# First layer's conditioning weights in pieces of 512 columns, and a charge for narrow tiles in the order planner

## The chip, the core and the metric

The kernel runs on one core of a Trainium2 chip: TensorE (PE, with its weight loads as PEld), VectorE (DVE), ScalarE (ACT), GpSimd (POOL) and SyncE (SP), which issues all DMAs. The metric is the device time of one execution in microseconds (us), the median of three runs.

## What is computed

Two layers of a hybrid mixer over 128 context tokens and 512 latent tokens, model width 2048, all in float32. The part that matters here is the start of a layer:

```python
mod_lat = (jax.nn.silu(c) @ w_ada[l] + b_ada[l])     # w_ada[l]: 2048 x 6144: shift, scale, gate
h = rmsnorm(x, norm_pre[l]) * (1.0 + scale) + shift
... = split_cols(h @ w_in[l])                        # 2048 x 6368
```

So `h`, and with it every product of the layer, waits for the scale and the shift, and these are a vector (one for context, one for latent tokens) times 2048 x 2048 weights each. What follows (a gated delta rule over 8 heads, latent attention over 4 heads, pooling over 4 groups, the output projection) is untouched by the change.

## The kernel before

**Order.** Every instruction is first recorded by `Sched.record`, with a cost from `Sched.cost`, and then placed by `Sched.run`, a list scheduler: each engine takes the ready instruction of highest priority in a simulated time, and the order in which it took them is the order of the program on that engine. `either` leaves a choice between two engines, which the scheduler settles by whichever is free first (the rounding `copy` between ACT and DVE, the remainder `rest` between POOL and DVE). So a change of a cost moves instructions all over the program. All instructions are emitted from one line (L499 in the profile), hence groups are told apart by tiles.

**The start of layer 0.** `start` goes over the 2048 columns of scale (`kind` 1) and shift (`kind` 0) in pieces listed in `WSTART`: eight of 256 columns. A piece and kind is loaded in four DMAs of 512 KB, each four row blocks of 128 rows by 256 columns (rows of 1 KB), alternately into the tiles `aw0` (slabV) and `aw1` (slabW), four buffers each. There are 64 such loads; they are numbered 1 to 64 here in program order. `ada_rows` multiplies each row block: the stationary operand is the conditioning vector as 128 x 32, so a product uses only 32 of the 128 output columns of the array, and row block `i` writes rows `32*(i % 4)` of one PSUM bank. Four row blocks thus use four different quarters of the array. `ada_sum` evacuates the sums, transposes them (tag `hp0`, a single PSUM bank) and adds up the four quarters; `mod_cols` makes `acl` and `bcl` from them. After the first piece the tokens `x` are loaded and normalised (`xnorm`), and for each 128 columns `k` of a finished piece `h_tile` transposes the tokens on PE (also in bank `hp0`), scales and shifts them (ACT or DVE) and splits them into a rounded part and a remainder. `consts2`, called after the first piece, transposes the convolution weights and small norms, in the same bank `hp0`; its last transposition (128x20) needs the small load `pool_scale`.

**Work beside it.** The first projections (`win_group` with tag `ax`, six PSUM banks) run over the blocks `k` as they become ready: products of 384 and of 256 columns in fp32r, called wide here. Everything else of the layer follows these.

Of the kernel before, what the change touches and what calls it, by code (L numbers as in the profile page):

```python
# [17 lines left out]
D = 2048  # L18
NK = 16
# [22 lines left out]
DK_EPS = 128 * EPS  # L42
RW = 24384
WW = {"W": 4096, "V": 4480}
WSTART = (256,) * 8
SW = 20248


# [103 lines left out]
def cols(x):  # L152
    n = 1
    for s in x.shape[1:]:
        n *= s
    return n


class Sched:
# [190 lines left out]
    def run(self):  # L350
        self.prepare()
        ev = []
        seq = 0
        engs = ["PE", "DVE", "ACT", "POOL", "SP"]
        free = {e: True for e in engs}
        heap = {e: [] for e in engs}
        hw = 0.0
        bus = 0.0
        last, warm, port = -10.0, 0.0, 0.0

        def push(o):
            for e in {o.eng, *o.alts}:
                heapq.heappush(heap[self.ENG[e]], (o.pr, o))

        for op in self.ops:
            if op.need == 0:
                push(op)
        now = 0.0
        done = 0
        order = []  # L370
        again = []

        def retry(tags):
            for g in tags:
                for o in g.waiting.pop(g.next, ()):
                    o.parked = False
                    push(o)

        every = [g for g in self.tags.values() if g.space != "D"]
        while True:  # L380
            for e in engs:
                while free[e] and heap[e]:
                    pr, op = heapq.heappop(heap[e])
                    if op.placed or op.parked:
                        continue
                    new = [t for t in op.tiles if t.slot is None]
                    miss = None
                    for t in new:
                        if not self.grant(t):
                            miss = t  # L390
                            break
                        if t.tag.space != "D":
                            again.append(t.tag)
                    if miss is not None:
                        op.parked = True
                        miss.tag.waiting.setdefault(miss.n, []).append(op)
                        continue
                    op.placed = True
                    if self.ENG[op.eng] != e:
                        (op.eng, op.meth, op.a, op.k, op.cost, op.lock), = [(n, *x) for n, x in op.alts.items() if self.ENG[n] == e]  # L400
                    op.start = now
                    op.seq = len(order)
                    order.append(op)
                    if op.meth == "dma_start":
                        hw = max(hw, now) + 0.45
                        op.bus = max(bus, hw)
                        bus = op.bus + op.nbytes / 340e3
                        op.end = max(bus, hw + 0.3) + 2.0
                    else:
                        cost = op.cost  # L410
                        if e == "PE":
                            if now - last > 3.4:
                                warm = now + 3.4
                            if now < warm:
                                cost *= 2
                            last = now + cost
                        op.end = now + cost
                        if op.lock:
                            op.end = max(now, port) + cost
                            port = op.end  # L420
                    free[e] = False
                    heapq.heappush(ev, (now + op.cost if op.meth == "dma_start" else op.end, 0, seq, e))
                    heapq.heappush(ev, (op.end, 1, seq, op))
                    seq += 1
            if again:
                retry(again)
                again = []
                if any(free[e] and heap[e] for e in engs):
                    continue
            if not ev:  # L430
                break
            now = ev[0][0]
            rel = False
            while ev and ev[0][0] <= now + 1e-9:
                _, kind, _, x = heapq.heappop(ev)
                if kind == 0:
                    free[x] = True
                elif kind == 1:
                    done += 1
                    eng = self.ENG[x.eng]  # L440
                    for t in x.tiles:
                        t.left -= 1
                        if t.left == 0 and t.tag.space != "D":
                            heapq.heappush(ev, (now + self.FREE[t.tag.space], 3, seq, t))
                            seq += 1
                    for s in x.succ:
                        s.need -= 1
                        lat = self.LAT["DMA" if x.meth == "dma_start" else eng][self.ENG[s.eng]]
                        s.ready = max(s.ready, now + lat)
                        if s.need == 0:  # L450
                            heapq.heappush(ev, (s.ready, 2, seq, s))
                            seq += 1
                elif kind == 3:
                    g = x.tag
                    g.used[x.slot] = None
                    x.dead = True
                    while g.low < len(g.tiles) and g.tiles[g.low].dead:
                        g.low += 1
                    rel = True
                else:  # L460
                    push(x)
            if rel:
                retry(every)
        if done != len(self.ops):
            waits = [(o.i, o.eng, o.meth, [t.tag.name for t in o.tiles if t.slot is None]) for o in self.ops if not hasattr(o, "end") and o.need == 0]
            raise RuntimeError(f"stuck: {done} of {len(self.ops)}: {waits[:5]}")
        self.order = order
# [34 lines left out]
class Body:  # L502
# [5 lines left out]
    def memory(self):  # L508
# [41 lines left out]
                       ("T1", 1, 160), ("T2", 1, 320), ("rv", 2, 128), ("Z", 4, 128), ("kg", 2, 128), ("s", 5, 128), ("dj2", 1, 128)], SW)  # L550
        put("S", fix, [("xy", 5, 2048), ("of", 2, 640), ("junk", 1, 512), ("ssy", 1, 25), ("zb", 6, 1), ("zh", 6, 1), ("zb4", 3, 4), ("gr3", 1, 384), ("G", 2, 1024), ("xr", 3, 512)], SW)
        put("S", at("gr3"), [("sq", 1, 256)], SW)
        st = [("r", 2, 128), ("th", 1, 128), ("ao", 1, 256), ("at3", 1, 4)]
        put("S", SW - sum(n * w for _, n, w in st), st, SW)
        put("S", SW - 260, [("ao2", 1, 256), ("at4", 1, 4)], SW)
        r4 = [at("raw") + 512 * i for i in range(4)]
# [112 lines left out]
    def start(self):  # L669
        nc, a = self.nc, self.a  # L670
        self.x1d = [[self.dram([128, 1024]) for _ in range(2)] for _ in range(NT)]
        r = self.T("r", [96, 128])
# [3 lines left out]
        p = self.ps("hp0")  # L676
# [6 lines left out]
        c0 = 0  # L683
        for s, w in enumerate(WSTART):
            ks = slice(c0 // 128, (c0 + w) // 128)
            n = w // 128
            for kind in (1, 0):
                p = self.ps("ad")
                for kc in range(4):
                    w4 = self.T(f"aw{kc % 2}", [128, 4, w])  # L690
                    nc.sync.dma_start(w4, a["w_ada"][0, kc * 512:(kc + 1) * 512, kind * D + c0:kind * D + c0 + w].rearrange("(k p) n -> p k n", p=128))
                    self.ada_rows(p, w4, kc * 4, kc == 0, kc == 3)
                t2 = self.T("at3", [128, n, 2])
                self.ada_sum(t2, p, self.T("ao", [128, w]), "hp0")
                self.mod_cols(0, kind, ks, t2, acl, bcl)
            if s == 0:
                for t in range(NT):
                    x = self.T("xy", [128, D])
                    nc.sync.dma_start(x, a["x_prompt"][0] if t == 0 else a["x_sample"][0, (t - 1) * 128:t * 128, :])
                    self.xt.append(x)  # L700
                for t in range(NT):
                    self.xnorm(t)
            for k in range(ks.start, ks.stop):
                self.h_tile(0, k, acl, bcl, "hp0")
            if s == 0:
                self.consts2()
            c0 += w
# [746 lines left out]
            nc.vector.scalar_tensor_tensor(szc[:, o0:o0 + n], p[:, :n], self.misc[:, 12 + 4 * l + g:13 + 4 * l + g], szc[:, o0:o0 + n], op0=ALU.mult, op1=ALU.mult)  # L1454
        nc.sync.dma_start(self.od[12 + g], szc)

    def ada_rows(self, p, w, k0, start, stop):

        nc = self.nc
        n = w.shape[1]  # L1460
        for i in range(n):
            j = i % 4
            with nc.later(-20 if i else 0):
                nc.tensor.matmul(p[32 * j:32 * j + 32, :w.shape[2]], self.ccol[:, 2 * (k0 + i):2 * (k0 + i) + 32], w[:, i], start=start and i < 4, stop=stop and i >= n - 4)

    def ada_sum(self, dst, p, o, pst):

# [8 lines left out]
    def ada_cols(self, l, i0, i1, tag, pst, m=1):  # L1476

        nc, a = self.nc, self.a
        for i in range(i0, i1, m):
# [3 lines left out]
            p = self.ps(pst)  # L1483
            for j, w in enumerate(ws):
                with nc.later(-20 if j else 0):
                    self.ada_rows(p[:, 128 * j:128 * j + 128], w, 0, True, True)
            with nc.later(-2):
                s = self.T("at4", [128, m, 2])
                self.ada_sum(s, p, self.T("ao2", [128, 128 * m]), pst)
# [177 lines left out]
```

## Time and profile before

| | us |
|---|---|
| median of three runs (2635.53 to 2638.45) | 2635.76 |
| profiled execution, own time | 2642.71 |
| profiled execution, span of its instructions | 2640.6 |
| PE busy in that span | 2541.0 (96%) |
| DVE, ACT, POOL busy | 1664.4, 1026.8, 739.7 |
| DMA, mean rate over the span; in the first 66 us | 132 GB/s; 314 GB/s |

A busy time is the sum of an engine's instructions, and PE counts as busy while a product is in its pipeline. The profile shows 40 slices of 66 us: PE is at 40% in the first one and at 90% or more in nearly all others; DMA is at 90% or more in the first two and far lower later.

### The profile page before, as it was taken

How to read it: one execution, taken by the hardware profiler on the slowest of the kernel's cores; microseconds unless marked ns; L12 is line 12 of the kernel's file. 1: busy time of each engine (PE TensorE's matmuls, PEld its weight loads, DVE VectorE, ACT ScalarE, POOL GpSimd, SP SyncE). 2: the span in 40 equal slices, each digit the busy share in tenths (PEclk: the TensorE clock that was granted, in tenths of full speed). 3: DMA queues.
4: the chain of work that ended last, by engine and by line, in shares of the span. 5: the costliest groups of instructions: out<-in, count | busy, mean ns of one | idle time of the engine just before them, and what ended most of it. 6: DMA issues, size and time to landing. Idle time of an engine off the chain costs nothing.

```text
span 2640.6 us, 52982 instructions
## 1 busy us (share of the span) xinstructions
PE 2541.0 (96%) x20553; PEld 2380.4 (90%) x20553; DVE 1664.4 (63%) x4229; ACT 1026.8 (39%) x2789; POOL 739.7 (28%) x825
## 2 busy tenths in 40 slices
PE   4999999999999999999988999999999999999998
PEld 1689999999999998878888999999999999988888
DVE  3545556888888886332257365678878887755225
ACT  3233345444444432222247333444444444323222
POOL 0021112354333333220025211233444333334002
PEclk7999999999999999999998999999999999999999
DMA  9944444332343333896755434523433334336225
GB/s 314 335 108 110 133 116 121 96 95 83 92 103 101 102 91 100 235 271 173 190 182 157 126 95 126 149 78 91 101 103 90 91 92 103 84 84 194 92 75 191
DMA packets 541202, 347.98 MB, mean 132 GB/s; under 512 B 103826, under 2 KB 499734, under 8 KB 540310
## 3 DMA queue, kind: packets, MB, share of 16 engines
q1 hardware_dynamic: 540950, 344.59, 46.7%
q8 instruction: 162, 2.65, 0.4%
q14 instruction: 90, 0.74, 0.1%
HBM read 313.07 MB, written 31.46 MB: 130 GB/s over the span
## 4 chain that ended last, share of the span: by engine, by line
PE 80%; DMA 6%; DVE 3%; ACT 2%; POOL 1%; issue 1%; SPq 1%; DVEq 0%; ACTq 0%
PE psum L499 80%; DVE slab L499 3%; DMA slab<-d 2%; DMA slab<-in_w_in_dram 1%; DMA slab<-in_w_ada_dram 1%; ACT slab L499 1%; POOL slabr L499 1%; DMA slabW<-in_w_ada_dram 1%; DMA d<-slab 1%; SPq L499 1%; ACT slabr L499 1%; ACT slabW L499 0%; DMA slab<-in_x_sample_dram 0%; DVE slabV L499 0%; DMA slabW<-d 0%
## 5 line engine op out<-in xcount | busy, mean ns | idle before, releaser
L499 PE MATMUL psum<-slabr 128*128 128x384 f32 (+2 forms) x11760 | 2011.1, 324 | 2.3 <-DVE slabW L499 1.0
L499 PEld LDWEIGHTS psum<-slabr 128*128 128x128 f32 x11760 | 1778.2, 190 | 86.9 <-issue 23.5
L499 POOL TENSOR_TENSOR slabr<-slab,slabr 128x512 fp32r<-128x512 f32 (+3 forms) x428 | 482.8, 1136 | 1200.3 <-ACT slabr L499 878.8
L499 ACT ACTIVATE slabr<-slab 128x512 fp32r<-128x512 f32 (+3 forms) x731 | 393.3, 548 | 879.2 <-PE psum L499 726.5
L499 DVE TENSOR_TENSOR slabr<-slab,slabr 128x512 fp32r<-128x512 f32 (+3 forms) x404 | 262.8, 654 | 416.1 <-ACT slabr L499 363.8
L499 PE MATMUL psum<-slab 128*128 128x128 f32 (+4 forms) x4375 | 434.7, 256 | 56.7 <-DVE slab L499 31.9
L499 DVE TENSOR_TENSOR slab<-slab 128x5 f32<-128x5 f32 (+20 forms) x1298 | 473.2, 376 | 19.2 <-DMA slab<-d 3.9
L499 ACT ACTIVATE slab<-psum 128x128 f32<-128x128 f32 (+6 forms) x823 | 276.1, 351 | 492.5 <-PE psum L499 384.7
L499 PEld LDWEIGHTS psum<-slab 128*128 128x128 f32 (+4 forms) x4375 | 352.1, 140 | 97.5 <-DVE slab L499 39.3
L499 DVE SCALAR_TENSOR_TENSOR slab<-slab 128x5 f32<-128x5 f32 (+7 forms) x618 | 348.2, 572 | 42.9 <-ACT slab L499 33.9
L499 ACT ACTIVATE slab<-slab 128x642 f32<-128x642 f32 (+4 forms) x240 | 141.1, 603 | 62.3 <-DVE slab L499 55.7
L499 DVE COPY slab<-psum 32x160 f32<-32x160 f32 (+9 forms) x214 | 84.0, 399 | 112.7 <-PE psum L499 98.0
L499 DVE TENSOR_SCALAR slab<-slab 128x1 f32<-128x1 f32 (+7 forms) x363 | 111.4, 326 | 29.0 <-ACT slabW L499 16.2
L499 POOL TENSOR_SCALAR slab<-slabV,slab 128x128 f32<-128x128 f32 x128 | 58.1, 460 | 217.5 <-PE psum L499 216.9
L499 DVE SCALAR_TENSOR_TENSOR slab<-psum,slab 128x128 f32<-128x128 f32 (+1 forms) x216 | 80.1, 378 | 56.4 <-PE psum L499 54.5
L499 DVE TENSOR_REDUCE slab<-psum 128x4 f32<-128x16 f32 (+3 forms) x104 | 39.5, 380 | 106.5 <-PE psum L499 105.3
L499 PE MATMUL psum<-slab,slabW 32*32 32x32 f32 (+2 forms) x1216 | 80.8, 219 | 14.5 <-DMA slab<-d 7.8
L499 POOL TENSOR_TENSOR slab<-slab 128x640 f32<-128x640 f32 (+5 forms) x46 | 68.1, 1481 | 95.1 <-ACT slab L499 77.8
L499 ACT ACTIVATE slab<-psum,slab 128x256 f32<-128x256 f32 (+2 forms) x93 | 58.7, 641 | 78.3 <-DVE slab L499 74.6
L499 PEld LDWEIGHTS psum<-slab,slabW 32*32 32x32 f32 (+2 forms) x1216 | 66.3, 132 | 23.1 <-DMA slab<-d 10.7
L499 DVE SCALAR_TENSOR_TENSOR slab<-slab,psum 128x128 f32<-128x128 f32 (+2 forms) x160 | 62.0, 395 | 37.2 <-PE psum L499 25.9
L499 PE MATMUL psum<-slab,slabV 128*128 128x128 f32 (+1 forms) x352 | 72.4, 296 | 1.9 <-DVE slab L499 1.4
(61 smaller groups left out, 1384.5 us busy)
## 6 DMA issues: line engine op xcount, KB each, us to landing
slab<-in_w_in_dram SPq DMA_DIRECT2D x186, 512.0 KB
slab<-in_w_ada_dram SPq DMA_DIRECT2D x32, 1024.0 KB
slabW<-in_w_ada_dram SPq DMA_DIRECT2D x32, 1024.0 KB
slab<-in_w_out_dram SPq DMA_DIRECT2D x64, 512.0 KB
slabW<-d SPq DMA_DIRECT2D x64, 320.0 KB
slabV<-in_w_ada_dram SPq DMA_DIRECT2D x32, 512.0 KB
slabW<-in_w_ada_dram SPq DMA_DIRECT2D x32, 512.0 KB
d<-slab SPq DMA_DIRECT2D x32, 320.0 KB
```

The source lines that it names most:

```text
L499: op.inst = getattr(getattr(nc, op.eng), op.meth)(*[real(x) for x in op.a], **{n: real(x) for n, x in op.k.items()})
```

## The change

`WSTART` becomes three pieces of 512 columns and two of 256. A load stays at 512 KB: for a piece of 512 columns it holds two row blocks (rows of 2 KB) and there are eight per kind, for one of 256 it holds four, as before. The number of loads stays 64; the first 48 are of the new form. `ada_rows` takes the row block's number instead of start and stop flags, so the two row blocks of one load write quarters 0 and 1 or quarters 2 and 3. `ao` and `at3` grow to 512 columns. In `Sched.run` a product on PE counts as narrow when its stationary operand has under 128 rows or 32 columns; a step to a narrow one is charged 0.1 us more, a step back 0.27 us.

```diff
-WSTART = (256,) * 8
+WSTART = (512, 512, 512, 256, 256)
...
                         if e == "PE":
+                            part = op.a[1].shape[0] < 128 or cols(op.a[1]) == 32
+                            if part != narrow:
+                                cost += 0.1 if part else 0.27
+                            narrow = part
...
-        st = [("r", 2, 128), ("th", 1, 128), ("ao", 1, 256), ("at3", 1, 4)]
+        st = [("r", 2, 128), ("th", 1, 128), ("ao", 1, 512), ("at3", 1, 8)]
...
-                for kc in range(4):
-                    w4 = self.T(f"aw{kc % 2}", [128, 4, w])
-                    nc.sync.dma_start(w4, a["w_ada"][0, kc * 512:(kc + 1) * 512, kind * D + c0:kind * D + c0 + w].rearrange("(k p) n -> p k n", p=128))
-                    self.ada_rows(p, w4, kc * 4, kc == 0, kc == 3)
+                m = 1024 // w
+                for i, k in enumerate(range(0, NK, m)):
+                    w4 = self.T(f"aw{i % 2}", [128, m, w])
+                    nc.sync.dma_start(w4, a["w_ada"][0, k * 128:(k + m) * 128, kind * D + c0:kind * D + c0 + w].rearrange("(k p) n -> p k n", p=128))
+                    self.ada_rows(p, w4, k)
...
-    def ada_rows(self, p, w, k0, start, stop):
+    def ada_rows(self, p, w, k0):
...
-            j = i % 4
+            j = (k0 + i) % 4
             with nc.later(-20 if i else 0):
-                nc.tensor.matmul(p[32 * j:32 * j + 32, :w.shape[2]], self.ccol[:, 2 * (k0 + i):2 * (k0 + i) + 32], w[:, i], start=start and i < 4, stop=stop and i >= n - 4)
+                nc.tensor.matmul(p[32 * j:32 * j + 32, :w.shape[2]], self.ccol[:, 2 * (k0 + i):2 * (k0 + i) + 32], w[:, i], start=k0 + i < 4, stop=k0 + i >= NK - 4)
```

The order of PE's instructions shows what this does to the loads' products. The row with `slabV` or `slabW` and a first size of 32 is one load; `slabr` rows are wide products, `slab 128x128` are transpositions. First, PE before, from ahead of load 15 to load 17:

```order
L499 MATMUL psum<-slab 128x120
L499 MATMUL psum<-slabV_78,slab 32x256 x4
L499 MATMUL psum<-slab 128x120
L499 MATMUL psum<-slabW_80,slab 32x256 x4
L499 MATMUL psum<-slabr 128x384 x2
L499 MATMUL psum<-slabr 128x256 x2
L499 MATMUL psum<-slabr 128x384 x6
L499 MATMUL psum<-slabr 128x256 x4
L499 MATMUL psum<-slabr 128x384 x4
L499 MATMUL psum<-slab 128x20
L499 MATMUL psum<-slab 128x128 x2
L499 MATMUL psum<-slabV_78,slab 32x256 x4
```

The last row is load 17: the first 18 wide products stand between loads 16 and 17, and the transposition of 20 rows, which waits for `pool_scale`, behind them. PE in the change, from load 16 (the first row) to load 21:

```order
L503 MATMUL psum<-slabW_80,slab 32x512 x2
L503 MATMUL psum<-slab 128x128 x4
L503 MATMUL psum<-slabV_78,slab 32x512 x2
L503 MATMUL psum<-slabW_80,slab 32x512 x2
L503 MATMUL psum<-slab 128x128 x3
L503 MATMUL psum<-slabV_78,slab 32x512 x2
L503 MATMUL psum<-slab 128x128 x2
L503 MATMUL psum<-slabW_80,slab 32x512 x2
L503 MATMUL psum<-slabr 128x384 x3
L503 MATMUL psum<-slab 128x128 x3
L503 MATMUL psum<-slabV_78,slab 32x512 x2
```

The first wide product stands behind load 20 now; loads 17 and 18 follow each other without anything between, the others here do not. PE in the change, from load 31 to the transposition of 20 rows, which now stands between loads 32 and 33:

```order
L503 MATMUL psum<-slabV_78,slab 32x512 x2
L503 MATMUL psum<-slabr 128x384 x4
L503 MATMUL psum<-slabW_80,slab 32x512 x2
L503 MATMUL psum<-slabr 128x384 x4
L503 MATMUL psum<-slabr 128x256 x12
L503 MATMUL psum<-slabr 128x384 x12
L503 MATMUL psum<-slab 128x20
```

Its load follows load 35 on SP (before: load 22). Counted over PE's whole order: before load 64 is multiplied, 120 wide products of 384 columns and 116 of 256 stand in the order before, 100 and 98 in the change; from load 16 to load 64 there are 87 transpositions and other small products before and 95 in the change; steps from wide to narrow and back come to 74 before and 80 in the change in that stretch, and to 253 and 251 in all that follows load 64. Of the 32 loads of 512 columns that follow load 16, six stand in three groups with a partner next to them (17 and 18; two of 33 to 35; two of 36 to 38). On the other engines 36 remainders of weights move from DVE to POOL.

## Rows read from the trace of the kernel before

**Rows 1.** The page: span, and busy time of each engine.

```profile
span 2640.6 us, 52982 instructions
...
PE 2541.0 (96%) x20553; PEld 2380.4 (90%) x20553; DVE 1664.4 (63%) x4229; ACT 1026.8 (39%) x2789; POOL 739.7 (28%) x825
```

**Rows 2.** Windows: stretch, its length, busy by engine (count), granted clock, DMA share, GB/s.

```profile
0.00:49.00 49.00, 20.76 (x137) 5.77 (x137) 21.00 (x84) 23.32 (x57) 0.47 (x6) 0.72 0.96 321
49.00:67.00 18.00, 11.35 (x77) 6.79 (x73) 3.51 (x12) 3.08 (x6) 2.88 (x5) 0.71 0.97 294
67.00:118.00 51.00, 51.00 (x468) 35.83 (x466) 26.40 (x71) 11.23 (x24) 1.71 (x2) 1.00 1.08 335
118.00:139.00 21.00, 19.10 (x181) 11.34 (x180) 12.94 (x32) 4.48 (x10) 2.79 (x3) 1.00 0.76 233
...
170.00:1020.00 850.00, 838.10 (x7093) 820.11 (x7092) 619.24 (x1609) 358.71 (x1027) 269.14 (x298) 1.00 0.38 102
...
1400.00:2320.00 920.00, 911.37 (x7607) 893.66 (x7606) 663.49 (x1678) 407.90 (x1134) 313.69 (x355) 1.00 0.39 102
```

**Rows 3.** Timeline of PE, 46 to 66 us: start, length, instruction, idle before it.

```profile
49.41 0.64 PE L499 MATMUL psum<-slabW,slab 128*32 128x256 f32 x8
50.37 3.08 PE L499 MATMUL psum<-slabr 128*128 128x384 f32 x18 [0.32 <-ACT slabr L499]
58.98 0.26 PE L499 MATMUL psum<-slab 20*128 20x20 f32 x1 [5.53 <-DMA slab<-in_pool_scale_dram]
```

**Rows 4.** Timeline of PE, 67 to 70 us (x8 is one load, two passes each).

```profile
67.12 0.64 PE L499 MATMUL psum<-slabV,slab 128*32 128x256 f32 x8
67.69 0.44 PE L499 MATMUL psum<-slab 128*128 128x128 f32 x2
68.06 0.64 PE L499 MATMUL psum<-slabW,slab 128*32 128x256 f32 x8
68.52 0.61 PE L499 MATMUL psum<-slabV,slab 128*32 128x256 f32 x8
68.95 0.61 PE L499 MATMUL psum<-slabW,slab 128*32 128x256 f32 x8
69.49 0.55 PE L499 MATMUL psum<-slab 128*128 128x128 f32 x3
69.80 0.42 PE L499 MATMUL psum<-slabr 128*128 128x384 f32 x1
```

**Rows 5.** Timeline of PE: load 64, and wide products after it.

```profile
138.15 0.64 PE L499 MATMUL psum<-slabW,slab 128*32 128x256 f32 x8
...
148.53 14.82 PE L499 MATMUL psum<-slabr 128*128 128x384 f32 x96 [0.58 <-ACT slabr L499]
```

**Rows 6.** Timelines of all engines: `ada_sum` after load 4, `pool_scale`'s issue, `h_tile`.

```profile
14.04 0.38 ACT L499 ACTIVATE slab<-psum 128x256 f32<-128x256 f32 x1 [8.52 <-PE psum L499]
...
15.61 0.16 DVE L499 SCALAR_TENSOR_TENSOR slab<-slab 128x4 f32<-128x4 f32 x1
...
52.67 0.29 SPq L499 DMA_DIRECT2D slab<-in_pool_scale_dram  x1
...
66.02 0.41 DVE L499 TENSOR_SCALAR slab<-psum,slab 128x128 f32<-128x128 f32 x1 [2.13 <-PE psum L499]
...
67.46 0.56 DVE L499 TENSOR_TENSOR slabr<-slab,slabr 128x384 fp32r<-128x384 f32 x1
```

**Rows 7.** Windows: loads with rows of 8 KB, then of mostly 1 KB.

```profile
20.00:28.00 8.00, 0.91 (x3) 0.38 (x3) 3.13 (x14) 6.44 (x18) 0.00 (x0) 0.61 1.01 420
90.00:100.00 10.00, 10.00 (x85) 6.89 (x85) 6.33 (x17) 1.58 (x4) 1.71 (x2) 1.00 1.11 338
```

**Rows 8.** Waits of PE from 139 us to the end: total, times, longest.

```profile
PE psum L499 <- DVE slab L499: 15.5, 12, 5.1
PE psum L499 <- ACT slab L499: 13.8, 6, 6.9
PE psum L499 <- DMA slab<-d: 7.8, 10, 1.4
```

More of the change, by code (lines that the diff above doesn't have):

```diff
@@ L358, in run @@
         bus = 0.0
-        last, warm, port = -10.0, 0.0, 0.0
+        last, warm, port, narrow = -10.0, 0.0, 0.0, False
         def push(o):
@@ L1485, in ada_cols @@
                 with nc.later(-20 if j else 0):
-                    self.ada_rows(p[:, 128 * j:128 * j + 128], w, 0, True, True)
+                    self.ada_rows(p[:, 128 * j:128 * j + 128], w, 0)
             with nc.later(-2):
```

## The prediction

> **What bounds the kernel now.** I read the page first: PE is busy for 2541.0 of 2640.6 us [rows 1], so a change is worth what it takes from PE's work or from PE's waits. Then the windows, to see where PE waits [rows 2]. In the first 49 us it is busy for 20.8 us; from 49 to 67 us for 11.4 of 18.0; from 67 to 118 us for all of 51.0; from 118 to 139 us for 19.1 of 21.0. In the long stretches of the two layers it lacks 11.9 of 850 and 8.6 of 920 us.
>
> The stretch from 67 to 118 us decides here. DMA runs there at a share of 1.08 and 335 GB/s, which looks like a start that waits for its weights. But "busy" alone does not say who leads, so I priced PE's work. One load costs 0.44 us of PE (68.06 to 68.95 us for two) [rows 4]. A wide product costs 0.153 us (14.65 us, the length less its last pipeline depth, over 96, half of 384 columns and half of 256) [rows 5]. A transposition costs 0.11 us (three from 69.49 to 69.80). A step to narrow products and back costs about 0.25 us: load 68.95 ends 0.54 us later rather than 0.44, and 67.69 to 68.06 is 0.37 us for two transpositions of 0.22 [rows 4]. From load 16 at 49.41 us [rows 3] to load 64 at 138.15 us [rows 5] are 88.7 us. PE's order has there 48 loads (21.1 us), 236 wide products (36.1), 87 small ones (9.6) and 37 steps there and back (9.3): 76.1 us of work, and 12.6 us of waits and half clock. Of these the 20-row transposition that waits for pool_scale is 5.53 us [rows 3], the granted clock of 0.71 from 49 to 67 us [rows 2], that is, partly at 1.2 GHz, costs some 2 to 3, and 118 to 139 us lacks 1.9. Between 67 and 118 us nothing is left to wait for. So **PE, not DMA, bounds the start from 67 us on**, and after load 64 its backlog of wide products goes on.
>
> **The change part by part.**
>
> *Loads up to 16.* The first eight loads, the tokens and the next eight loads stand in the same order on SP as before; only now all sixteen belong to the first piece. PE waits for them in both kernels. A load of 512 KB takes 1.55 us at 338 GB/s (rows of mostly 1 KB) and 1.25 us at 420 GB/s (rows of 8 KB) [rows 7]. No row shows a saturated queue with rows of 2 KB, so the saving is between 0 and 0.30 us per load; I take 0.12, nearer to the 1 KB rows, because 2 KB is. The eight loads before load 16 then give -0.9 us (0 to -2.4). Other SP entries of this stretch do not move.
>
> *Products of loads of 512 columns.* Before, a load's four row blocks use four quarters of the array at once: 0.44 us for 256 columns. Now a load's two row blocks use two quarters, for 512 columns each: twice the length, 0.88 us, with half of the array idle. The other two quarters could take the next load, but only if it is next on PE. Of the 32 such loads after load 16, six stand in three groups with a partner beside them, so 29 lengths of 0.88 remain: 25.5 us for what cost 14.1. No row shows two quarters alone. Lower bound: nothing more than now, if a pass with half the quarters ran twice as fast; the single full-width transpositions (128 columns, 0.11 us a pass) speak against that, since their pass is as long per column as that of four quarters. Upper bound: the partners do not overlap either, 2.6 us more.
>
> *Work from load 16 to load 64.* In the change: 25.5 us, 16 loads of 256 columns (7.0), 198 wide products (30.3), 95 small ones (10.5), 40 steps there and back (10.0): 83.3 us against 76.1. The 38 wide products that are no longer done by load 64 come later: 38 x 0.153 + 4 transpositions of 0.11 = +6.2, less one step there and back (-0.2): +6.0.
>
> *Waits in that stretch.* Before, 12.6 us. What becomes of them? (a) After load 16 the scale and shift must be made: 1.73 us from the evacuation's start to the last operation for 256 columns [rows 6], some 2.3 for 512 (ACT's 0.38 doubles, two more transpositions); then 2.0 us from scaling to the remainder [rows 6], and about 0.5 us of hand-over on either side. So the first wide product can start some 6.2 us after load 16. PE has loads 16 to 20 and the small products before it, 5.3 us: a wait of 1 to 2 us. (b) The 20-row transposition now stands behind load 32, some 34 us of work after load 16, at about 86 us. Its small load follows load 35 on SP; that one needs the buffer of load 27, which PE leaves after some 20 us of work, near 71 us. Before, it landed 6.3 us after its issue at 52.67 us [rows 3, 6]. So it lands near 79 us and the 5.5 us should be gone; what is late next is PE's own work. (c) The clock: PE runs the loads 9 to 16 without a gap of its own now and goes on, so the half-clock part should shrink; I keep 1 us. (d) The 1.9 us near 120 us I keep at 1. Sum 4 us, between 2 and 7.
>
> *Larger `ao`, fewer sums.* ACT and DVE lie beside PE at 11.2 and 26.4 us of 51.0 [rows 2]: nothing.
>
> *The planner's charge.* It issues no instruction. It moves the order in the rest by small amounts, and 36 remainders from DVE to POOL. The number of steps there stays (253 to 251). What it can win are PE's waits behind 139 us, of which the three largest kinds are 15.5, 13.8 and 7.8 us [rows 8]; the longest, 6.9 and 5.1 us, are at the seam of the layers, where PE's order is the same in both kernels. The rest is spread in pieces of about a microsecond. I take 0, between -5 and +5.
>
> **Sum**, against the profiled execution: -0.9 (loads) + 83.3 + 4.0 - 88.7 (stretch: -1.4) + 6.0 (later) + 0 = +3.7 us, its span to 2644.3. The profiled execution's own time of 2642.71 is 7 us above the median, which moves by the same amount: 2635.8 + 3.7 = **2639.5 us**.
>
> **The rivals.**
>
> *The stretch waits as before.* The half-array products come and the waits stay: if the small load lands behind the 20-row transposition at 86 us, as it does now, the bank `hp0` is held and all later sums with it. Waits of 10 instead of 4 us: 2645.5 us, slower. For it: the wait exists today with the same bank and the same kind of order. Against: the load now has 15 us from its issue, not 6.3.
>
> *The start is DMA-bound after all.* Then 48 loads gain 0.12 to 0.30 us each, 6 to 14, and PE follows: 2622 to 2630 us. For it: the share of 1.08 [rows 2]. Against: 51.0 us without a wait, and PE's work adds up by itself. The Trainium skill, Perfetto Trace Analysis, DMA Optimizations, says that small DMAs, under 2 KB, carry much overhead and that larger ones are the first remedy when a kernel is DMA-bound; by it this rival would hold. The rows agree on the rate (338 to 420 GB/s), but not that the stretch waits for DMA.
>
> *The charge pays in the rest.* If the better-planned order saves half of the spread waits of both layers, 8 us, the total is 2631.5 us; a little more and it is faster.
>
> *The new order costs in the rest.* 36 remainders of weights are now made by POOL instead of DVE; POOL is busy for 269 of 850 us, DVE for 619 [rows 2], so it has the room, but each tile of weights waits for its remainder. If each of the 36 holds PE for 0.2 us, a value of the size of the spread waits, the sum grows by 7: 2646.5 us.
>
> **How the numbers follow.** One part in 500, 5.3 us, is about what a measurement tells from no change: faster is under 2630.5, slower over 2641.0. My forecast, with its bounds (-2.4 to 0, 2 to 7 us of waits, partners, the rest), covers 2634 to 2645, so a quarter of it lies on the slow side. Chances: forecast 0.50, waits stay 0.18, DMA-bound 0.08, charge pays 0.12 (half of it over the bound), order costs 0.12. Slower: 0.11 + 0.18 + 0.10 = 0.39; faster: 0.07 + 0.06 = 0.13; the same: 0.48. The range leaves out a tenth on either side: 2629 to 2648 us.
>
> **What would show it.** In the profile of the changed kernel: a load's two row blocks should last about 0.88 us on PE from 50 us on; no wait for pool_scale; load 64 at about 136 us (134 to 141) with PE busy without gaps from some 57 us; the DMA rate in the second 66 us lower, since PE holds the buffers. If load 64 comes near 125 us, DMA was the bound. If two half-array loads take 0.88 us together wherever they stand, my largest term is wrong. If the layers' middle stretches differ by more than 5 us, the planner's charge is what decided.

## The result: 2668.3 us, 1.2 per cent slower

| | before | after |
|---|---|---|
| median of the runs on one chip, us | 2635.65 | 2668.30 (2662.66 to 2671.76) |
| ratio, 95% interval | | 1.0119 [1.0101, 1.0138] |
| profiled execution, own time / span, us | 2642.71 / 2640.6 | 2662.66 / 2660.9 |

The change costs 32.6 us; I had forecast +3.7 and a range that ends at 2648. The profiled execution of the change is the fastest of its four and that of the kernel before is above its median, so the two traces differ by 20.3 us only.

The page of the kernel after, against [rows 1] (span, then busy time by engine):

```profile
span 2660.9 us, 52545 instructions
...
PE 2552.6 (96%) x20361; PEld 2374.8 (89%) x20361; DVE 1670.4 (63%) x4164; ACT 1023.2 (38%) x2792; POOL 786.6 (30%) x866
```

Windows of the kernel after, the stretches of [rows 2] (length, busy PE, PEld, DVE, ACT, POOL, granted clock, DMA share, GB/s):

```profile
0.00:49.00 49.00, 20.86 (x74) 3.78 (x74) 16.86 (x71) 22.67 (x55) 1.31 (x7) 0.83 0.94 338
49.00:67.00 18.00, 17.88 (x93) 8.23 (x92) 10.88 (x26) 3.16 (x6) 2.13 (x3) 1.00 1.06 376
67.00:118.00 51.00, 50.84 (x308) 27.08 (x308) 19.11 (x50) 9.26 (x17) 4.08 (x6) 1.00 0.96 316
118.00:139.00 21.00, 20.90 (x182) 15.12 (x179) 14.21 (x35) 8.25 (x16) 2.80 (x3) 1.00 0.60 181
...
1400.00:2320.00 920.00, 898.49 (x7488) 877.26 (x7489) 659.98 (x1664) 409.11 (x1133) 327.68 (x363) 0.99 0.40 105
```

The first 139 us look better than before: from 49 to 67 us PE is busy for 17.9 us instead of 11.4, at the full 2.4 GHz (clock 1.00 instead of 0.71). Part of the loss stands in the last row: PE lacks 21.5 of 920 us there, where it lacked 8.6.

Waits of PE from 139 us to the end, kernel after, against [rows 8] (total, times, longest):

```profile
PE psum L503 <- DVE slab L503: 18.8, 16, 5.0
PE psum L503 <- DMA slab<-d: 15.4, 13, 2.7
PE psum L503 <- ACT slab L503: 11.4, 6, 6.6
PE psum L503 <- DMA slabW<-in_w_ada_dram: 9.8, 13, 2.5
```

The wait for `slab<-d` has doubled, from 7.8 us. `d` is scratch memory in DRAM: each of the 16 heads solves a triangular system on VectorE in 31 steps, writes the result there in four DMAs, reads it back in nine in another layout, and only then come its small products on PE (32x32 and 64x64).

To see where the time is lost, I compared when the same product (the n-th of its form) starts in the two traces. After minus before: +1.4 us at 190 us, when the start is over; +1.0 at the first 64x64 product of layer 0 (517 us); +15.4 at the last one (1055 us); +12.8 in layer 0's output projection; +17.5 at layer 1's first 64x64 product; +20.3 in its output projection. **The start costs one microsecond, the heads of the two layers nearly all the rest.**

### The profile page after: what moved, and what is told of

It is laid out like the page before. It is cut to its first block, busy times and chain, and to the rows that moved or that the text cites. A ratio compares the mean times of both kernels' runs of the same rounds, so it can differ in the third digit from the quotient of the medians.

```text
span 2660.9 us, 52545 instructions
## 1 busy us (share of the span) xinstructions
PE 2552.6 (96%) x20361; PEld 2374.8 (89%) x20361; DVE 1670.4 (63%) x4164; ACT 1023.2 (38%) x2792; POOL 786.6 (30%) x866
## 4 chain that ended last, share of the span: by engine, by line
PE 80%; DMA 11%; DVE 5%; SPq 2%; ACT 1%; issue 1%; POOL 0%; DVEq 0%; ACTq 0%; POOLq 0%
PE psum L503 80%; DVE slab L503 4%; DMA slabW<-in_w_ada_dram 3%; DMA slab<-d 2%; SPq L503 2%; DMA slab<-in_w_ada_dram 1%; DMA slab<-in_w_in_dram 1%; DMA d<-slab 1%; ACT slab L503 1%; DMA slabW<-d 1%; DMA d<-slabV 0%; DMA slab<-in_x_prompt_dram 0%; POOL slabr L503 0%; DMA slab<-in_x_sample_dram 0%; ACT slabr L503 0%
## 5 line engine op out<-in xcount | busy, mean ns | idle before, releaser
L503 POOL TENSOR_TENSOR slabr<-slab,slabr 128x512 fp32r<-128x512 f32 (+3 forms) x470 | 529.4, 1136 | 1165.6 <-ACT slabr L503 976.7
L503 DVE TENSOR_TENSOR slabr<-slab,slabr 128x512 fp32r<-128x512 f32 (+3 forms) x362 | 248.5, 691 | 408.5 <-ACT slabr L503 379.3
L503 DVE TENSOR_TENSOR slab<-slab 128x5 f32<-128x5 f32 (+20 forms) x1292 | 481.5, 384 | 24.3 <-DMA slab<-d 9.0
L503 ACT ACTIVATE slab<-psum 128x128 f32<-128x128 f32 (+8 forms) x811 | 272.0, 352 | 521.8 <-PE psum L503 418.6
L503 DVE SCALAR_TENSOR_TENSOR slab<-slab 128x5 f32<-128x5 f32 (+8 forms) x615 | 353.4, 583 | 57.0 <-ACT slab L503 52.5
L503 DVE COPY slab<-psum 32x160 f32<-32x160 f32 (+7 forms) x220 | 88.1, 407 | 112.9 <-PE psum L503 102.4
L503 POOL TENSOR_SCALAR slab<-slabV,slab 128x128 f32<-128x128 f32 x128 | 65.3, 518 | 235.9 <-PE psum L503 235.4
L503 DVE TENSOR_SCALAR slab<-slab 128x1 f32<-128x1 f32 (+9 forms) x368 | 118.5, 342 | 21.8 <-ACT slabW L503 11.1
L503 PE MATMUL psum<-slab,slabW 32*32 32x32 f32 (+2 forms) x1216 | 81.5, 221 | 21.1 <-DMA slab<-d 15.4
L503 DVE TENSOR_REDUCE slab<-psum 128x1 f32<-128x640 f32 (+4 forms) x98 | 38.5, 393 | 82.4 <-PE psum L503 81.8
L503 DVE SCALAR_TENSOR_TENSOR slab<-slab,psum 128x128 f32<-128x128 f32 (+2 forms) x160 | 62.3, 396 | 34.4 <-PE psum L503 21.5
L503 PE MATMUL psum<-slabW,slab 128*32 128x128 f32 (+2 forms) x1184 | 65.3, 312 | 11.3 <-DMA slabW<-in_w_ada_dram 11.0
```

Of the source, the lines that this page charges most:

```text
L503: op.inst = getattr(getattr(nc, op.eng), op.meth)(*[real(x) for x in op.a], **{n: real(x) for n, x in op.k.items()})
```

## Experiments

Times are medians of the runs; "before" was run beside each on the same chip (2637 to 2640 us). All edits are to the changed kernel unless said otherwise. In its planner, `part` says whether a product is narrow, `cost` is the simulated duration.

### One half of the change at a time

```diff
-                                cost += 0.1 if part else 0.27
+                                cost += 0.0
```

> The pieces of 512 columns alone, the charge set to zero. Theory (the charge reorders the rest and costs all of it; the start is worth nothing in the end): 2634 to 2642 us, load 64 near 134 us as in the change, and the milestones of layer 0 from 1030 to 1176 us within 3 us of the kernel before. Rival (the pieces leave the planner in another state after the start and that reshuffles the rest): 2655 to 2670 us. In the planner's order only 51 of PE's 16886 later instructions stand elsewhere than in the kernel before, which speaks for the theory.

```diff
-WSTART = (512, 512, 512, 256, 256)
+WSTART = (256,) * 8
```

> The charge alone, with eight pieces of 256 columns as before. Theory: 2655 to 2672 us, with the same loss near 1034 to 1176 us and in the heads of layer 1 as in the change. Rival (the charge does nothing, the pieces cost): 2633 to 2640 us.

Measured: pieces alone 2649.45 us, ratio 1.0040 [1.0025, 1.0055]; charge alone 2677.93 us, 1.0141 [1.0124, 1.0158]. The charge costs nearly all, as the theory has it, and more than expected. But the pieces alone are not free: load 64 comes at 147 us, and all of their 10 us (2649.45 against 2639.57) are lost in the start (in the trace +12.3 at 190 us, +10.9 at 517, +7.3 at the end). The timeline of PE, pieces alone (start, length, instruction, idle before it), shows how:

```profile
131.19 0.55 PE L503 MATMUL psum<-slab 128*128 128x128 f32 x3 [0.63 <-DVE slab L503]
133.15 0.44 PE L503 MATMUL psum<-slab 128*128 128x128 f32 x2 [1.42 <-ACT slab L503]
134.79 0.69 PE L503 MATMUL psum<-slab 128*128 128x128 f32 x2 [1.20 <-DVE slab L503]
135.95 1.08 PE L503 MATMUL psum<-slabV,slab 128*32 128x256 f32 x8 [0.47 <-ACT slab L503]
```

Transpositions follow one another through the single bank `hp0` with no wide products left between them: the planner had used these up too early. So the charge has two effects: it saves about 10 us in the start and costs some 30 behind it.

### Is it the start, or the price of a load?

```diff
-                                cost += 0.1 if part else 0.27
+                                cost += (0.1 if part else 0.27) if now < 140.0 else 0.0
```

> The change with the charge made only in the first 140 us of the planner's time. Theory (the charge repairs the plan of the start, where a load of 512 columns is priced at 0.45 us and takes about 0.98, and spoils the order of the heads): load 64 near 134 us as in the change, the rest as with the pieces alone, 2632 to 2640 us, that is no change against the kernel before on the same chip within 0.2 per cent. Rival (the start's gain of some 10 us and the loss later belong together, since wide products done early are missing as cover later): 2645 to 2660 us.

Measured: 2640.71 us, 1.0002 [0.9993, 1.0012]; load 64 at 133.9 us, no milestone of the rest over 4 us from before. Start and rest can be had apart.

```diff
-                return 0.01 + n / 2400
+                return 0.01 + n / (1200 if n == 512 else 2400)
```

with the charge at zero:

> The pieces of 512 columns, no charge at steps; instead the planner's price of one conditioning product of 512 columns is doubled, from 0.22 to 0.44 us, since two of them were seen to take about 0.98. Theory (in the start the charge only makes up for this wrong price): load 64 at 133 to 138 us, not 147, and the total 2634 to 2642 us, no change against the kernel before. Rival (the steps themselves have to be in the plan of the start): load 64 later than 142 us and the total 2645 to 2652 us.

Measured: 2637.08 us, 0.9990 [0.9977, 1.0003]; load 64 at 132.4 us. In the start the charge only stands in for the wrong price of a half-array product.

### Which charge, how much of it, or any new order?

```diff
-                            part = op.a[1].shape[0] < 128 or cols(op.a[1]) == 32
+                            part = op.a[1].shape[0] < 128
```

> The change, but only stationary operands with under 128 rows count as narrow (the solves of the heads); the conditioning products with 32 columns are not charged. Theory (the conditioning loads of layer 1 come late because their products are charged): about 2648 to 2656 us, with the waits for the conditioning weights of layer 1 gone, that is the 13 us between 1034 and 1176 us gone. Rival (the solves' charge brings the new order of the heads and with it the loss): 2660 to 2672 us.

Measured: 2670.50 us, 1.0133 [1.0102, 1.0164]. The rival is right: the solves' charge is enough. Of its +27.5 us in the trace, +10.6 are the start, since conditioning is not charged.

```diff
-                            part = op.a[1].shape[0] < 128 or cols(op.a[1]) == 32
+                            part = op.a[1].shape[0] == 128 and cols(op.a[1]) == 32
```

> The change, but only stationary operands of 32 columns (conditioning) count as narrow, not the heads' solves. Theory (the solves' charge spoils the heads, as the kernel with that charge alone had all of the loss): start as in the change, heads within 3 us of the kernel with the charge in the first 140 us alone, total 2634 to 2645 us. Rival (the late conditioning of layer 1 comes from its own charge): a loss of 8 to 13 us between the last head of layer 0 and its output projection, total 2648 to 2655 us.

Measured: 2648.07 us, 1.0036 [1.0025, 1.0048]. I had this wrong: conditioning's charge has a loss of its own, +10.4 us in the trace, all of it in layer 0 between 914 and 1176 us.

Half and double charge (0.05 and 0.13; 0.2 and 0.54):

> The change with half the charge (0.05 and 0.13 us). Theory (the charge pushes the heads' chain back in proportion): half of the loss in the rest, 10 to 14 us, and a start between the two seen (0 to 10 us later than before): 2645 to 2662 us. Rival (each set of costs gives one of many orders, good or bad without regard to size): anywhere from 2630 to 2675 us, with a loss in the rest under 5 or over 18 us.

> The change with the double charge (0.2 and 0.54 us). Theory (in proportion): start within 5 us of the change, loss in the rest 35 to 50 us, total 2675 to 2695 us. Rival (an order drawn without regard to size): loss in the rest under 30 us.

Measured: 2651.58 us, 1.0050, and 2681.64 us, 1.0163. In the traces the loss behind 190 us is 3.7 us for half, 18.9 for the whole and 32.8 for the double charge: it grows with the charge, but not in proportion; half fits the rival, and the double charge lies between both ranges.

```diff
-                        cost = op.cost
+                        cost = op.cost * (1.015 if e == "PE" else 1.0)
```

with the charge at zero:

> The pieces of 512 columns with no charge for narrow products; instead every cost on PE is 1.5 per cent higher in the planner, which lengthens its plan by about as much and moves about as many of PE's later instructions (2659 instead of 2585). Theory (the charge, since it is put on the narrow steps, makes the order worse): 2634 to 2645 us. Rival (any new order of the rest costs some 20 to 30 us, because the order before is a good one by chance or by choice): 2655 to 2670 us.

Measured: 2644.36 us, 1.0016 [1.0007, 1.0025]; start +12.1 us, rest -9.9. So it is not any new order that costs: this one moves as many products and wins 9.9 us in the rest. Joined with the early charge (flat factor from 140 us on):

> The change with the charge only in the first 140 us of the planner's time, and from there 1.5 per cent on every cost of PE in the planner. Theory (start and rest add up: start of the change +1, rest of the flat plan -9 us against the kernel before): 2625 to 2635 us, faster than both kernels. Rival (parts do not add up): 2637 to 2650 us.

Measured: 2633.82 us, 0.9980 [0.9970, 0.9990], faster than both kernels; the parts add up.

### Through what does the charge cost?

I measured in each trace the heads' chain: from the end of a head's solve on VectorE to its first small product (the trip through DRAM; sum over 16 heads), and from the first solve's start to the end of the last head's 64x64 products.

| kernel | trips, us | chain, layer 0 / layer 1, us | median, us |
|---|---|---|---|
| before | 155.9 | 601.3 / 602.9 | 2635.65 |
| early charge | 156.7 | 602.9 / 601.2 | 2640.71 |
| early charge, flat factor | 153.8 | 596.3 / 599.1 | 2633.82 |
| the change | 184.1 | 616.1 / 611.9 | 2668.30 |
| solves charged only | 183.6 | 617.9 / 613.4 | 2670.50 |
| charge with 256-column pieces | 186.3 | 622.4 / 620.5 | 2677.93 |

The change's chains are 23.8 us longer, its trips 28.2 us. In the traces the span less both chains is 1433 to 1437 us in all six kernels, so what they differ by stands in the chains. First, I shortened the solve, with and without the charge; this leaves out 15 of its 31 steps (the expectations' 16 are the steps that stay):

```diff
-        for j in range(31):
+        for j in range(0, 31, 2):
```

> The change, with 16 of the 31 steps of each head's triangular solve on VectorE left out (so part of the computation is missing in all 16 heads). Theory (the charge costs through the serial chain of the heads: solve on VectorE, round trip through memory, small products, so the last head and all behind it come late): with the chain shortened this loss goes, and the kernel stands within 6 us of its partner without the charge, less the 10 us that the charge gains in the start, so -10 to -4 us against it. Rival (the charge costs PE time by itself, through more work at steps or a lower clock): still some 12 us slower than the partner.

> The partner of the kernel with the shortened solve: the pieces of 512 columns without the charge, 16 of the 31 steps of each solve left out. Theory: PE bounds the heads here too, so 2625 to 2645 us, at most some 15 us under the pieces alone; slower than the shortened kernel with the charge by 4 to 10 us. Rival: faster than that one by some 12 us.

Measured: 2644.11 and 2647.33 us; 2635.0 and 2639.3 us in the traces. With the solve shortened the charge is no longer a loss: 3 to 4 us faster, just short of the 4 to 10 expected and within the scatter of the two (2636.8 to 2662.5, 2641.1 to 2650.3), where it was 13 to 19 us slower with whole solves. That fits a loss through the chain, but doesn't show it: the trips are 161.1 us with the charge here and 167.3 without, so the shorter solve also made an order in which the charge doesn't lengthen them. And without the charge, chains that are 63 us shorter than those of the pieces alone (1139.4 against 1202.7) make the span only 8.6 us shorter.

Then the queue. The timeline around the trip of layer 0's last head, in the change (DVE's row is the solve's last step, SPq SyncE's DMAs, four of the first five writes those of the solve, idle time in brackets):

```profile
1042.84 1.04 DVE L503 COPY slab<-slab 40x1024 f32<-40x1024 f32 x1
1043.21 12.19 PE L503 MATMUL psum<-slabr 128*128 128x256 f32 x80
...
1044.66 2.12 SPq L503 DMA_DIRECT2D d<-slab  x5
1046.88 0.88 SPq L503 DMA_DIRECT2D slab<-in_w_in_dram  x1
1047.85 3.63 SPq L503 DMA_DIRECT2D slab<-d  x6
1051.59 1.10 SPq L503 DMA_DIRECT2D slab<-in_w_in_dram  x1
1053.78 2.35 SPq L503 DMA_DIRECT2D slab<-d  x3
...
1058.10 1.09 PE L503 MATMUL psum<-slab,slabW 32*32 32x32 f32 x40 [2.70 <-DMA slab<-d]
```

The same with the early charge only:

```profile
1037.80 1.03 DVE L503 COPY slab<-slab 40x1024 f32<-40x1024 f32 x1
...
1040.29 4.86 SPq L503 DMA_DIRECT2D slab<-d  x9
1041.95 4.75 PE L503 MATMUL psum<-slabr 128*128 128x256 f32 x32
...
1046.63 0.73 PE L503 MATMUL psum<-slab,slabW 32*32 32x32 f32 x40
...
1049.18 1.13 SPq L503 DMA_DIRECT2D slab<-in_w_in_dram  x2
```

In the change a load of weights of 512 KB stands ahead of the solve's nine reads and another among them; here such loads follow them. The trip lasts 14.2 us instead of 7.8. PE fills it with 80 wide products instead of 32 and still waits 2.70 us, and then the 40 small products take 1.09 us instead of 0.73: from 1058 to 1068 us the granted clock is 0.50, that is 1.2 GHz, where it was 1.00 from 1044.5 us to the wait. The Trainium skill, DMA: Bandwidth & Descriptors, Queues, rings and completion order, says that SP has one ring on each DMA engine and that descriptors are consumed there in ring order; by that rule, reads wait for a load issued ahead of them, and the trace agrees: the first read lands 6.6 us after its issue here (1047.85 to 1054.40), 2.7 us with the early charge (1040.29 to 1042.96).

This head is the longest trip, and in others the load acts earlier. The head before it in the change, SyncE's DMAs and its longest wait from 973 to 987 us (the solve ends at 974.53 us, the trip lasts 13.1 us, with the early charge 10.8):

```profile
973.37 1.83 SPq L503 DMA_DIRECT2D d<-slab  x4
979.12 0.39 SPq L503 DMA_DIRECT2D slab<-in_w_in_dram  x1
979.62 1.00 SPq L503 DMA_DIRECT2D slab<-d  x2
```

```profile
SPq L503 <- POOL slab L503: 3.9, 1, 3.9
```

SyncE stands for 3.9 us at a load whose buffer POOL has still to free, and the reads behind it on SyncE wait with it. Over the 16 heads, from a solve's first write to its last read, there are 12 loads of 512 KB in the change, and 10 also in the kernel before and with the early charge. What grew is less their number than their price: after the ends of the solves, SyncE stands for 18.4 us at such loads in the change and for 8.7 with the early charge.

But such rows alone are no proof, so I let the planner hold back large loads during a trip (edit shortened):

```diff
+                    if e == "SP" and away > 0 and now < until and op.nbytes >= 1 << 18 and not op.trip:
+                        held.append(op)
...
+                    if op.trip == 1:
+                        away += 9 / 4
+                        until = now + 8.0
+                    elif op.trip == 2:
+                        away -= 1
+                        if away <= 0:
...
```

`trip` is 1 on the four writes and 2 on the nine reads of a solve; what is held goes on when the reads are placed, or after 8 us.

> The change, and in the planner a load of 256 KB or more is held back on the queue of SyncE from the solve's first write to its last read (8 us at most). Theory (the charged order puts weight loads ahead of the solve's reads, and the round trip is late for that): the round trips come to 155 to 170 us over 16 heads, and the kernel is 8 to 20 us faster than the change on the same chip. Rival (the round trip is late because the small products stand later on PE): round trips stay over 178 us, and the time within 5 us of the change.

> The change itself, beside the kernel that holds loads back, on the same chip: 2660 to 2672 us by all theories.

Measured: 2632.78 us, 0.9975 [0.9965, 0.9985] against before; the change beside it 2671.73 us. The hold takes 39 us from the change, more than I expected, and makes it faster than the kernel before. No such load is left in a trip; trips 150.2 us (the change here: 186.7), chains 595.5 / 597.0. The page of the kernel with the hold, and its SyncE around the last head of layer 0:

```profile
span 2629.5 us, 52504 instructions
...
PE 2538.6 (97%) x20361; PEld 2366.7 (90%) x20361; DVE 1672.3 (64%) x4186; ACT 1021.4 (39%) x2792; POOL 763.6 (29%) x844
```

```profile
1031.33 6.11 SPq L524 DMA_DIRECT2D slab<-d  x9
1037.54 0.38 SPq L524 DMA_DIRECT2D d<-slab  x1
1038.03 0.40 SPq L524 DMA_DIRECT2D slab<-in_w_in_dram  x1
```

Does the hold undo the charge's loss, or is it worth that with any order? The hold with the early charge only, and with charge and 256-column pieces:

> The hold of loads of 256 KB or more during a solve's round trip, with the charge in the first 140 us of the planner's time alone. Theory (the uncharged order of the heads has no such collisions of weight, so the hold has little to undo): within 4 us of the kernel with the early charge alone, 2634 to 2643 us. Rival (the hold is worth as much with any order): 2625 to 2632 us, or below.

> The charge and the hold with eight pieces of 256 columns, as before. Theory (the charge's loss goes with the hold here too, and the pieces are worth nothing in the end): 2630 to 2639 us, within 4 us of the same with pieces of 512 columns. Rival: the loss of the charge alone, 2655 us or more.

Measured: 2631.65 us, 0.9964 [0.9951, 0.9978], and 2630.65 us, 0.9965 [0.9951, 0.9979]; trips 146.9 and 147.3 us. I was wrong on the first: the hold gains 9 us without the late charge too (trips from 156.7 to 146.9). So it does both. With the hold, the late charge costs 1 us (2632.78 against 2631.65); without it, 28 to 31. And the pieces of 512 columns are worth nothing (2632.78 against 2630.65).

## Why the prediction was wrong, point by point

The timeline of PE in the kernel after, against [rows 3 to 5]:

```profile
46.65 1.05 PE L503 MATMUL psum<-slabW,slab 128*32 128x512 f32 x4 [0.37 <-DMA slabW<-in_w_ada_dram]
...
49.20 0.62 PE L503 MATMUL psum<-slabV,slab 128*32 128x512 f32 x2
49.61 0.62 PE L503 MATMUL psum<-slabW,slab 128*32 128x512 f32 x2
...
50.59 0.55 PE L503 MATMUL psum<-slab 128*128 128x128 f32 x3
...
65.85 1.05 PE L503 MATMUL psum<-slabW,slab 128*32 128x512 f32 x4
66.83 0.62 PE L503 MATMUL psum<-slabr 128*128 128x384 f32 x2
...
82.36 0.23 PE L503 MATMUL psum<-slab 20*128 20x20 f32 x1
...
85.39 0.62 PE L503 MATMUL psum<-slabV,slab 128*32 128x512 f32 x2
85.41 0.62 PE L503 MATMUL psum<-slabW,slab 128*32 128x512 f32 x2
85.85 0.60 PE L503 MATMUL psum<-slabV,slab 128*32 128x512 f32 x2
85.86 0.60 PE L503 MATMUL psum<-slabW,slab 128*32 128x512 f32 x2
86.28 1.03 PE L503 MATMUL psum<-slabV,slab 128*32 128x512 f32 x4
...
134.03 0.64 PE L503 MATMUL psum<-slabW,slab 128*32 128x256 f32 x8
```

- **Loads up to 16: right in kind, too small.** Load 16 at 46.65 us instead of 49.41: -2.8, where I had -0.9 and at most -2.4. I had counted the gain of eight loads; load 9 is already issued 1.1 us earlier (32.54 instead of 33.60). And with rows of 2 KB the DMA moves 376 GB/s from 49 to 67 us, nearer to the middle of my two rows than I took it.
- **Half-array products: right.** A load alone takes 0.98 us to the next product (65.85 to 66.83; 0.88 forecast, without the step); two beside each other take 0.89 us together (85.39 to 86.28), pass by pass in turn. Loads 17 and 18 take 1.39 (49.20 to 50.59), as the second begins 0.41 us later. The Trainium skill, TensorEngine Tiling (Array Packing), Tiling Modes, says that tiles of 128x32 work independently of each other; the rows agree.
- **Load 16 to load 64: right in sum, in part by luck.** 87.4 us (46.65 to 134.03) against 83.3 + 4.0, but only 1.3 us of it are idle: 2.7 us less of waits and 2.8 us more of work cancel. The wait for pool_scale is gone (82.36 has none), load 64 comes at 134 us (forecast 136), and DMA's rate falls as said.
- **Later work: right.** The start ends 1.4 us later than before; -2.8 - 1.3 + 6.0 gives +1.9.
- **The planner's charge: wrong, and it is nearly the whole miss.** The step that failed is "It moves the order in the rest by small amounts", with "I take 0, between -5 and +5". It measured 28 us between medians (the change against the early charge alone: 2668.3 and 2640.7) and 20.0 between the traces. I had read sums: the count of steps, the net number of remainders that changed engine, the longest waits, the order at the seam. None of them shows the position of a load on SyncE against a solve's reads; with such loads held back, the late charge costs 1 us (2632.78 against 2631.65). My own test for this step, over 5 us in the layers' middle stretches, is what came out.
- **The bound.** I took PE's busy share as proof that PE bounds the layers. It is 98% in the heads of both kernels, yet 36.5 us less of trips (186.7 to 150.2) went with 39 us less of time. So in the change the heads' chain leads, and PE's work fills it. That isn't so in every order: the shortened solve without the charge took 63 us from the chains and 8.6 from the span, so there PE's work leads. And "busy" is not a fixed amount of work: with the hold PE's busy time falls from 2552.6 to 2538.6 us for the same 20361 products, at a mean granted clock of 0.992 instead of 0.987. By these, 13.6 of the 14.0 us are the clock's (an estimate: 1.3% of 2660.9 us less 0.8% of 2629.5).
- **The rivals.** "The new order costs in the rest" had the sign and the place, but a quarter of the price. Its carrier, PE waiting for remainders on POOL, is not in the waits: they hold 1.3 us for POOL. POOL comes in elsewhere, at the loads that SyncE holds until POOL frees their buffers; whether the 36 moved remainders make that later, no run separates. The start is not bound by DMA, nor did the waits stay.

What stays open: the losses with half the charge, the double one and conditioning's alone do not lie in the trips (154.8, 156.8 and 156.4 us, with 4, no and 10 loads of 512 KB in them), so the trips are the way of the charge's loss in this order, not in every one; the double charge's chains are 12.1 us longer than before all the same. From the last 64x64 product of layer 0 to its output projection these kernels take 128.1, 132.7 and 125.9 us, the kernel before 121.0; there conditioning weights of layer 1 are loaded, and no run separates that.

## What to carry to other kernels

A better price in a planner is not a better plan: this charge moved only the planner's clock, it never chose between products by it. Ask of a new order where the transfers of each serial chain stand on their in-order queue, and what stands ahead of them: keeping 512 KB loads out of the trips was worth 9 us in one order and 39 in another. A busy share of 98% doesn't exclude that a chain beside it sets the length; shorten the chain once in each order, and see.

## What I had not expected of the hardware

- Two loads that use different halves of the array can finish together in 0.89 us, no slower than one alone (0.98 us with its step).
- A wait of 2.70 us on PE was paid twice: the 40 small products behind it took 1.09 us instead of 0.73, at a granted clock of 0.50 from 1058 to 1068 us.
- Nine small reads are issued on SyncE within 4.86 us (6.11 with the hold) when nothing stands between them, and within 8.3 us (1047.85 to 1056.13) with one large load among them and a wait of 1.1 us for the load ahead of them to land.
